# Modulation rows moved between stages, and products queued between a norm's two TensorE steps

## The chip, the core and the metric

The kernel runs on one core of a Trainium2 chip. The metric is device time of one launch in microseconds (us). A core has TensorE (PE, matrix products), VectorE (DVE), ScalarE (ACT), GpSimd (POOL) and SyncE (SP, which here only issues DMA transfers); each takes its instructions in the order in which the program has them.

## What is computed

The reference is a two-layer decoder trunk on one sequence of 1024 positions with 1024 channels, in float32. Layer 0 mixes by multi-scale pooling, layer 1 by dilated attention over one shared key/value set; after each mixer stands a gated FFN. Every sub-layer has the form

```
mod = cond @ ada_w[layer] + ada_b[layer]              # cond = silu(c)
sh1, sc1, g1, sh2, sc2, g2 = jnp.split(mod, 6, axis=-1)
h = _rmsnorm(x, norm_g) * (1 + sc) + sh
x = x + g * mixer_or_ffn(h)
```

with `_conv_ffn`: `a, v = split(h @ w_up)`, a causal 3-tap convolution on `a`, `(silu(a) * v) @ w_down`, width 2816. The key/value set has its own shift and scale from `cond @ kv_ada_w`. So there are 14 modulation rows of 1024 numbers: 0 to 5 of layer 0, 6 to 11 of layer 1, 12 and 13 of the key/value norm.

## The kernel before

Products in float32 accuracy are made of three float32r products (`whi`·`hhi`, `whi`·`hlo`, `wlo`·`hhi`); ACT rounds a weight tile to its high part, DVE subtracts for the low part (`split`, L105 to L108). Activations lie channel by position in two chunks c = 0, 1 of 512 positions.

**Stages.** Pooling layer (to 287 us); first FFN, up phase (287 to 822 us) and down phase (to 1064 us); query projection (1076 to 1310 us); value projection (1310 to 1600 us); attention with the key projection and output projection between (to 2254 us); second FFN (2267 us to the end). The first FFN and the second are the same code (`Ffn`).

**Up phase.** 22 pairs of weight tiles (`Pair`), each product done by a Strassen-like scheme in seven blocks of 12 matrix products. For the first AHEAD = 8 pairs two of the seven, which need only chunk 0 of the input, are done first (`ahead`, into a tile `ah` of the pool `t4`, stored to `ed`); `late` then makes the other operands from chunk 1 (`Norm.apply`), and `rest` does the remaining blocks for each pair in turn. `gate` (L483 on) applies convolution and gate and stores the pair's result by a GpSimd DMA (`gd<-at`, L530): one such store per pair marks the end of that pair.

**Modulation rows 5 to 13.** Each is made by `ada_dot` (L313 on): for each of 8 blocks SP loads a 512 KB tile `araw` (L321), POOL multiplies it by the conditioning row `condr` (L322), and ACT sums it in four activations with an accumulator (L325). `bg_ada` finishes the row before and starts the next. Nine rows, 72 tiles, are put into the first up phase: `bgl` is called after pair 0 and after each odd pair. `araw`, `condr` and `ah` all come from `t4`, which has 3 buffers in the FFN stages and 4 in the value projection, where the result tiles `vt` use it too.

**Norms.** `Norm.rstd` (L198 on) sums squares over channels by eight one-column TensorE products `nps` (L201), takes the root with Newton's correction on DVE (`newton`), builds four diagonals `ndg`, and spreads them over the partitions by a second TensorE product `nrs` (L208), which ACT copies to `rs`. `down_last` (L383 on) does chunk 0 of the last down products, then rstd(0) and `apply` for chunk 0, spread among the products of chunk 1, then rstd(1).

**Order.** The instructions of each engine are not run in the order of the Python code: outside the blocks under `manual_schedule` a scheduler sorts them when the program is built, with the order of the code as a preference. The order that results is fixed in the program.

## Time and profile before

| | us |
|---|---|
| median of 3 runs | 2961.41 |
| lowest, highest | 2957.07, 2967.33 |
| profiled execution | 2962.21 |
| its span, first to last instruction | 2960.4 |
| PE busy | 2757.2 (93%) |
| DVE, ACT, POOL busy | 1871.3 (63%), 1197.1 (40%), 556.5 (19%) |

The span is what the trace covers; 1.8 us of the execution lie outside it. Busy shares are averages over stages that are limited by different engines, so a stage is read by its own stretch of the trace. A PE that is busy 50 of 50 us runs one product of 512 columns each 0.227 us; PEclk is the granted TensorE clock as a share of full speed. In a row of a timeline the bracket gives the idle time before the instruction and what ended it.

### The profile page before, as it was taken

The numbers are of one execution on the slowest core, as the hardware profiler recorded it, in microseconds if no ns is written. First come the engines' busy times: TensorE is split into PE (matmuls) and PEld (weight loads), VectorE is DVE, ScalarE is ACT, GpSimd is POOL, SyncE is SP. The second block draws the span as 40 slices with busy tenths as digits, with TensorE's granted clock in tenths as the row PEclk, the third lists the DMA queues.
The fourth block names the chain that finished last, engine by engine and source line by source line (L and its number), as shares of the span: only waits on it lengthen the run. The fifth ranks groups of instructions, "written<-read, shape, count | busy, mean of one in ns | idle before, by whom it ended". The sixth has DMA issues, their size and how long they took to land.

```text
span 2960.4 us, 38089 instructions
## 1 busy us (share of the span) xinstructions
PE 2757.2 (93%) x14220; PEld 2254.0 (76%) x14220; DVE 1871.3 (63%) x3215; ACT 1197.1 (40%) x2599; POOL 556.5 (19%) x454
## 2 busy tenths in 40 slices
PE   7988978888999989989999999999988999999997
PEld 4766766666888878879999776777666888888885
DVE  6897699987665476651011565655767896666554
ACT  4634455666421143332122444544444444443112
POOL 2565154555000020000000122222142000000001
PEclk9998989999999989999999999999998999999998
DMA  7434455554342234452232233333532442225221
GB/s 298 139 131 139 160 201 180 171 171 149 131 168 100 93 122 166 167 192 100 93 99 87 74 101 110 109 103 102 159 87 100 166 139 80 84 86 206 93 71 57
DMA packets 148681, 383.76 MB, mean 130 GB/s; under 512 B 15520, under 2 KB 53392, under 8 KB 148496
## 3 DMA queue, kind: packets, MB, share of 16 engines
q1 hardware_dynamic: 109728, 292.37, 29.7%
q10 hardware_dynamic: 26496, 50.34, 4.7%
q0 software_dynamic: 12272, 38.62, 4.0%
q8 instruction: 112, 1.84, 0.2%
q14 instruction: 73, 0.60, 0.1%
HBM read 295.22 MB, written 86.05 MB: 129 GB/s over the span
## 4 chain that ended last, share of the span: by engine, by line
PE 64%; DVE 17%; DMA 9%; issue 5%; ACT 3%; POOL 2%; SPq 0%; DVEq 0%; ACTq 0%; POOLq 0%
PE dps L339 6%; PE dps L340 5%; PE dps L341 5%; PE pX L412 5%; PE pX L413 5%; PE pX L414 5%; PE vps L990 3%; PE vps L988 3%; PE vps L989 3%; DVE at L501 2%; DVE wlo L108 2%; PE pY L412 2%; PE pY L414 2%; PE pY L413 2%; PE kps L339 2%
## 5 line engine op out<-in xcount | busy, mean ns | idle before, releaser
L108 DVE TENSOR_TENSOR wlo<-wraw,whi 128x1024 fp32r<-128x1024 f32 x164 | 214.6, 1315 | 296.1 <-ACT whi L107 295.5
L339 PE MATMUL dps<-slab,whi 128*128 128x512 f32 x832 | 329.1, 397 | 9.6 <-DVE x L375 7.4
L340 PE MATMUL dps<-slab,whi 128*128 128x512 f32 x832 | 326.0, 393 | 0.0
L341 PE MATMUL dps<-slab,wlo 128*128 128x512 f32 x832 | 323.8, 393 | 0.9 <-DVE wlo L108 0.9
L375 DVE SCALAR_TENSOR_TENSOR x<-dps,mods,x 128x512 f32<-128x512 f32 x280 | 203.1, 746 | 155.7 <-PE dps L341 152.2
L107 ACT ACTIVATE whi<-wraw 128x1024 fp32r<-128x1024 f32 x164 | 169.8, 1052 | 304.2 <-PE dps L340 189.7
L1161 ACT ACTIVATE ss<-ss,ngm 128x128 f32<-128x128 f32 (+1 forms) x384 | 168.0, 439 | 191.6 <-DVE ngm L1158 178.5
L322 POOL TENSOR_TENSOR araw<-araw,condr 128x1024 f32<-128x1024 f32 x72 | 194.8, 2712 | 213.1 <-DMA araw<-in_ada_t_dram 204.8
L988 PE MATMUL vps<-whi,h 128*128 128x256 f32 x768 | 218.3, 284 | 6.1 <-ACT h L225 6.1
L990 PE MATMUL vps<-whi,h 128*128 128x256 f32 x768 | 217.7, 285 | 2.5 <-DVE h L226 2.5
L989 PE MATMUL vps<-wlo,h 128*128 128x256 f32 x768 | 217.9, 284 | 0.0
L412 PE MATMUL pX<-ht,whi 128*128 128x512 f32 x448 | 180.0, 403 | 24.7 <-ACT at L518 10.5
L339 PEld LDWEIGHTS dps<-slab,whi 128*128 128x128 f32 x832 | 158.5, 190 | 47.7 <-DVE x L375 10.3
L501 DVE SCALAR_TENSOR_TENSOR at<-at,P 128x512 f32<-128x512 f32 (+2 forms) x176 | 178.9, 1021 | 12.7 <-ACT at L498 11.4
L341 PEld LDWEIGHTS dps<-slab,wlo 128*128 128x128 f32 x832 | 158.0, 190 | 34.5 <-DVE wlo L108 1.3
L340 PEld LDWEIGHTS dps<-slab,whi 128*128 128x128 f32 x832 | 158.5, 191 | 33.6 <-issue 1.0
L414 PE MATMUL pX<-ht,wlo 128*128 128x512 f32 x448 | 178.2, 399 | 3.9 <-DVE wlo L108 3.8
L413 PE MATMUL pX<-ht,whi 128*128 128x512 f32 x448 | 178.8, 399 | 0.0
L108 DVE TENSOR_TENSOR wlo<-s,whi 128x1024 fp32r<-128x1024 f32 x112 | 150.0, 1344 | 34.6 <-ACT whi L107 34.2
L107 ACT ACTIVATE whi<-s 128x1024 fp32r<-128x1024 f32 x112 | 117.7, 1057 | 122.2 <-PE pY L413 43.5
L339 PE MATMUL kps<-h,whi 128*128 128x512 f32 x384 | 166.1, 433 | 0.0
L988 PEld LDWEIGHTS vps<-whi,h 128*128 128x128 f32 x768 | 148.4, 193 | 6.7 <-ACT h L225 6.7
(256 smaller groups left out, 6642.7 us busy)
## 6 DMA issues: line engine op xcount, KB each, us to landing
wraw<-in_wup_dram SPq DMA_DIRECT2D x104, 512.0 KB, 3.7
araw<-in_ada_t_dram SPq DMA_DIRECT2D x72, 512.0 KB, 3.9
gd<-at POOLq DMA_DIRECT2D x44, 512.0 KB, 3.5
wraw<-gd SPq DMA_DIRECT2D x44, 512.0 KB, 3.4
wraw<-in_wdn_dram SPq DMA_DIRECT2D x44, 512.0 KB, 4.1
wraw<-in_wq_dram SPq DMA_DIRECT2D x32, 512.0 KB, 4.2
xd<-x ACTq DMA_DIRECT2D x48, 256.0 KB, 2.0
ed<-ah ACTq DMA_DIRECT2D x24, 512.0 KB, 3.8
```

Source lines behind the costliest of these rows:

```text
L107: nc.scalar.activation(hi, raw, AF.Copy)
L108: nc.vector.tensor_tensor(lo, raw, hi.bitcast(F32), op=ALU.subtract)
L339: nc.tensor.matmul(ps, whi, hhi, start=first, stop=False)
L340: nc.tensor.matmul(ps, whi, hlo, start=False, stop=False)
L341: nc.tensor.matmul(ps, wlo, hhi, start=False, stop=last)
L412: nc.tensor.matmul(ps, w[0][:, k], hh, start=start and j == 0, stop=False, **kw)
L413: nc.tensor.matmul(ps, w[0][:, k], hl, start=False, stop=False, **kw)
L414: nc.tensor.matmul(ps, w[1][:, k], hh, start=False, stop=j == 3, **kw)
L501: nc.vector.scalar_tensor_tensor(t[:, lo + o:hi], a[:, lo + o - d:hi - d], pc(cw, 22 * (2 - d) + i), t[:, lo + o:hi], op0=ALU.mult, op1=AL ...
L988: nc.tensor.matmul(o, a, whi[:, k], start=kt == 0, stop=False)
L989: nc.tensor.matmul(o, a, wlo[:, k], start=False, stop=False)
L990: nc.tensor.matmul(o, b, whi[:, k], start=False, stop=kt == KT - 1)
```

## The change

Two things. First, the rows: only row 5 stays in the first up phase (after pair 12, finished after pair 17). Rows 6, 7, 12 and 13 are called after the first four sets of the down phase, rows 8 to 11 in the value projection, before every second of its first ten column groups. `condr` is loaded twice (`load_condr`), where it is first needed. Second, `rstd` becomes a generator that stops between the Newton step and the second product. In `down_last` one block of chunk 1 is called between the two for chunk 0; for chunk 1 the generator goes to the caller, which steps it after its ahead products 0 and 1.

```diff
         def rstd(self, c):
+
             ps = nbank("nps")
...
                 nc.vector.tensor_scalar(dg[:, 128 * n:128 * n + 128], ident, r[:, n:n + 1], None, op0=ALU.mult)
+            yield
             ps = nbank("nrs")
...
-            return rs
+            yield rs
...
         down(*gb, x, g, (0,), norm)
-        ap = done(0, norm.rstd(0))
+
+        def steps(c):
+            r = norm.rstd(c)
+            next(r)
+            yield
+            yield from done(c, next(r))
+
+        ap = steps(0)
         for m, _ in enumerate(down_pieces(ga[0] + gb[0], ga[1] + gb[1], x, g, (1,), norm)):
-            if m >= LEAD:
+            if m in (0, 1) or m >= LEAD:
                 next(ap)
         for _ in ap:
             pass
-
-        r = norm.rstd(1)
-
-        def late():
-            for _ in done(1, r):
-                pass
-        return late
+        return steps(1)
...
-        def up(self, late, bg=()):
-            bg = list(bg)
+        def up(self, late, bg={}):
...
                 p.ahead(ed[self.l, i])
-            late()
+                if i < 2:
+                    next(late)
+            for _ in late:
+                pass
             for i, p in enumerate(ps):
                 p.rest(self.gate(i))
-                if bg and (i == 0 or i % 2 == 1):
-                    bg.pop(0)()
-            for b in bg:
-                b()
-
-        def down(self, norm, done):
+                if i in bg:
+                    bg[i]()
+
+        def down(self, norm, done, bg=()):
...
                     down(rhs, ws, x, mod(6 * l + 5))
+                    if n < len(bg):
+                        bg[n]()
...
-    bgl = [lambda i=i: bg_ada(i) for i in (5, 6, 7, 12, 13, 8, 9, 10, 11, None)]
-    condr = tp.tile([128, 1024], F32, tag="t4", name="condr")
-    nc.sync.dma_start(condr, cvec[0, :].partition_broadcast(128))
-    nc.scalar.activation(condr, condr, AF.Silu)
+    def bg_ada_list(ids):
+        return [lambda i=i: bg_ada(i) for i in ids]
+
+    def load_condr():
+        t = tp.tile([128, 1024], F32, tag="t4", name="condr")
+        nc.sync.dma_start(t, cvec[0, :].partition_broadcast(128))
+        nc.scalar.activation(t, t, AF.Silu)
+        return t
+
     f0 = Ffn(0, tp, hs1, SL0, xd[0], gd[0])
-    f0.up(late, bgl)
-    x, late = f0.down(nrm, done1)
+
+    def first_ada():
+        nonlocal condr
+        condr = load_condr()
+        bg_ada(5)
+
+    condr = None
+    f0.up(late, {12: first_ada, 17: lambda: bg_ada(None)})
+    x, late = f0.down(nrm, done1, bg_ada_list((6, 7, 12, 13, None)))
...
+        condr = load_condr()
+        bgl = bg_ada_list((8, 9, 10, 11, None))
         for cg in range(12):
+            if cg % 2 == 0 and cg < 10:
+                bgl[cg // 2]()
             w = [wprep(wv[cg, i]) for i in range(2)]
```

The query projection and the end of the kernel step `late` in the same way as `up`. What the scheduler makes of it stands in the two programs.

POOL in the first up phase. `araw` is a modulation tile's product, a `gd` row the store that ends a pair. Before, the stretch around the stores of pairs 14, 15 and 16:

```order
L530 DMA gd_555<-at_4547 128x1024
L322 TENSOR_TENSOR araw_4540<-araw_4540,condr 128x1024
L322 TENSOR_TENSOR araw_4815<-araw_4815,condr 128x1024
L322 TENSOR_TENSOR araw_4822<-araw_4822,condr 128x1024
L322 TENSOR_TENSOR araw_4829<-araw_4829,condr 128x1024
L322 TENSOR_TENSOR araw_4836<-araw_4836,condr 128x1024
L530 DMA gd_555<-at_4679 128x1024
L322 TENSOR_TENSOR araw_4843<-araw_4843,condr 128x1024
L322 TENSOR_TENSOR araw_4850<-araw_4850,condr 128x1024
L322 TENSOR_TENSOR araw_4857<-araw_4857,condr 128x1024
L322 TENSOR_TENSOR araw_4864<-araw_4864,condr 128x1024
L530 DMA gd_555<-at_4871 128x1024
```

There the last products stand ahead of the store of pair 16 (`at_4871`). POOL now, around the stores of pairs 9, 10 and 11:

```order
L533 DMA gd_555<-at_3412 128x1024
L324 TENSOR_TENSOR araw_6238<-araw_6238,condr 128x1024
L324 TENSOR_TENSOR araw_6245<-araw_6245,condr 128x1024
L324 TENSOR_TENSOR araw_6252<-araw_6252,condr 128x1024
L324 TENSOR_TENSOR araw_6259<-araw_6259,condr 128x1024
L324 TENSOR_TENSOR araw_6266<-araw_6266,condr 128x1024
L533 DMA gd_555<-at_3544 128x1024
L533 DMA gd_555<-at_3676 128x1024
```

Products stand before the stores of pairs 0 to 16 in the program before (6, 3, 3, 3, 4, 3, 4, 2, 5, 5, 5, 5, 5, 5, 5, 5 and 4: 72) and before those of pairs 0 to 10 in the changed one (5, 3, 3, 3, 3, 3, 5, 1, 6, 3 and 5: 40). These 40 are all five rows 5, 6, 7, 12 and 13: none of them lies among the products of the down phase, though the code calls four rows from there. The other 32 lie in the value projection.

PE at the norm of chunk 1 ahead of the query projection. `dps` is the last down product, `pX` an ahead product. Before:

```order
L341 MATMUL dps_7288<-slab_6964,wlo_6972 128x512
L201 MATMUL nps_7317<-ones,sq_7157 128x1
L201 MATMUL nps_7317<-ones,sq_7174 128x1
...
L208 MATMUL nrs_7339<-ndg_7334,ones 128x512
L412 MATMUL pX_7349<-hb_7196,whi_7345 128x512
```

There nothing stands between the last `dps`, the eight `nps` and `nrs`. PE now, the same place; the twelve rows of `pX_7086<-hb_6941`, of `pX_7143<-hb_6941`, of `pX_7086<-hb_6965` and of `pX_7143<-hb_6965` are shown by one each:

```order
L343 MATMUL dps_7055<-slab_6727,wlo_6735 128x512
L417 MATMUL pX_7086<-hb_6941,wlo_7083 128x512
...
L202 MATMUL nps_7115<-ones,sq_6894 128x1
L417 MATMUL pX_7143<-hb_6941,wlo_7140 128x512
...
L417 MATMUL pX_7086<-hb_6965,wlo_7083 128x512
L202 MATMUL nps_7115<-ones,sq_6933 128x1
...
L417 MATMUL pX_7143<-hb_6965,wlo_7140 128x512
L210 MATMUL nrs_7172<-ndg_7132,ones 128x512
L415 MATMUL pX_7205<-hb_6941,whi_7201 128x512
```

Four blocks of 12 products now stand ahead of `nrs` where none stood, and 12 of them ahead of the first `nps`. The norms ahead of the two up phases have the same pattern. For chunk 0 (three of the four norms) the 12 products of one block now lie between the first `nps` and the other seven; `nrs` still follows the last `nps` at once. The last norm of chunk 1, at the end of the kernel, is as it was.

SP at the start of the value projection; `hkx` is an input of the norm's second scaling, `wraw` a weight tile, `vslab` an input of the attention. Before, the last of the `hkx` loads and what follows:

```order
L971 DMA hkx_9095<-xd_553 128x512
L971 DMA hkx_9100<-xd_553 128x512
L971 DMA hkx_9105<-xd_553 128x512
L103 DMA wraw_9974<-in_wv_dram 128x1024
L103 DMA wraw_9980<-in_wv_dram 128x1024
L1034 DMA vslab_11733<-vd 128x8x128
```

There only weight tiles follow. SP now, the same place:

```order
L991 DMA hkx_8863<-xd_553 128x512
L323 DMA araw_8898<-in_ada_t_dram 128x1024
L991 DMA hkx_8868<-xd_553 128x512
L323 DMA araw_8905<-in_ada_t_dram 128x1024
L323 DMA araw_8912<-in_ada_t_dram 128x1024
L323 DMA araw_8919<-in_ada_t_dram 128x1024
L323 DMA araw_8926<-in_ada_t_dram 128x1024
L103 DMA wraw_9915<-in_wv_dram 128x1024
L103 DMA wraw_9921<-in_wv_dram 128x1024
```

Four modulation tiles now stand ahead of the next weight tiles; the tile before `hkx_8868`, three others and the conditioning row stand among the eight `hkx` loads of chunk 1.

## Rows read from the trace of the kernel before

**Rows 1.** Stretches, both up phases: PE, PEld, DVE, ACT, POOL busy (instructions), clock, DMA

```profile
287.00:823.00 536.00, 464.68 (x1886) 368.79 (x1885) 438.94 (x458) 306.12 (x834) 207.46 (x94) 0.94 0.49 165
...
2267.00:2697.00 430.00, 428.67 (x1885) 353.62 (x1884) 319.42 (x436) 193.58 (x258) 11.64 (x22) 1.00 0.34 117
```

**Rows 2.** Timeline of TensorE, first product of each ahead phase: start, duration

```profile
286.93 1.42 PE L412 MATMUL pX<-hb,whi 128*128 128x512 f32 x1
...
2266.67 1.42 PE L412 MATMUL pX<-hb,whi 128*128 128x512 f32 x1
```

**Rows 3.** Timeline of GpSimd, first FFN: stores of pairs 7, 10, 16, 21

```profile
511.13 0.58 POOL L530 DMA_DIRECT2D gd<-at  x1 [6.18 <-DVE at L528]
...
583.75 0.59 POOL L530 DMA_DIRECT2D gd<-at  x1
...
735.45 0.59 POOL L530 DMA_DIRECT2D gd<-at  x1 [3.90 <-DVE mods L330]
...
822.29 0.53 POOL L530 DMA_DIRECT2D gd<-at  x1 [18.20 <-DVE at L529]
```

**Rows 4.** Timeline of GpSimd, second FFN: stores of pairs 7, 10, 16, 21

```profile
2432.86 0.53 POOL L530 DMA_DIRECT2D gd<-at  x1 [9.73 <-DVE at L528]
...
2487.33 0.53 POOL L530 DMA_DIRECT2D gd<-at  x1 [18.69 <-DVE at L529]
...
2600.62 0.54 POOL L530 DMA_DIRECT2D gd<-at  x1 [18.78 <-DVE at L529]
...
2696.62 0.53 POOL L530 DMA_DIRECT2D gd<-at  x1 [18.38 <-DVE at L529]
```

**Rows 5.** Busy time per engine, two stretches of the first up phase

```profile
287.00:350.00 63.00, 57.29 (x239) 45.90 (x238) 44.87 (x61) 29.87 (x43) 0.00 (x0) 0.96 0.40 135
350.00:511.00 161.00, 130.15 (x501) 101.58 (x501) 147.69 (x151) 91.38 (x280) 81.00 (x35) 0.90 0.55 185
```

**Rows 6.** VectorE groups by shape, 400 to 740 us: count, busy, mean ns

```profile
L108 DVE TENSOR_TENSOR wlo<-s,whi 128x1024 fp32r<-128x1024 f32 x30 | 50.3, 1685 | 14.8 <-ACT whi L107 14.8
...
L501 DVE SCALAR_TENSOR_TENSOR at<-at,P 128x512 f32<-128x512 f32 x30 | 45.6, 1521 | 0.6 <-ACT at L498 0.5
```

**Rows 7.** The same two groups, 2400 to 2690 us (second FFN)

```profile
L108 DVE TENSOR_TENSOR wlo<-s,whi 128x1024 fp32r<-128x1024 f32 x29 | 35.4, 1220 | 2.1 <-ACT whi L107 2.1
...
L501 DVE SCALAR_TENSOR_TENSOR at<-at,P 128x512 f32<-128x512 f32 x30 | 22.4, 748 | 1.4 <-ACT at L498 1.0
```

**Rows 8.** The page's costliest groups: the modulation products on GpSimd

```profile
L322 POOL TENSOR_TENSOR araw<-araw,condr 128x1024 f32<-128x1024 f32 x72 | 194.8, 2712 | 213.1 <-DMA araw<-in_ada_t_dram 204.8
```

**Rows 9.** ScalarE groups, 350 to 740 us: the sums of those products

```profile
L325 ACT ACTIVATE araw<-araw 128x256 f32<-128x256 f32 x288 | 116.0, 404 | 71.0 <-POOL araw L322 63.1 <-DVE mods L329 6.1 <-DVE mods L330 1.8
L325 ACT ACTIVATION_READ_ACCUMULATOR araw<-araw 128x1 f32 x288 | 53.9, 187 | 0.0
```

**Rows 10.** Timeline of TensorE, norm ahead of the query projection, chunk 1

```profile
1063.64 0.39 PE L341 MATMUL dps<-slab,wlo 128*128 128x512 f32 x1
1066.14 0.38 PE L201 MATMUL nps<-ones,sq 128*128 128x1 f32 x2 [2.11 <-POOL sq L195]
1068.97 3.15 PE L201 MATMUL nps<-ones,sq 128*128 128x1 f32 x14 [2.44 <-DVE sq L195]
1074.53 2.07 PE L208 MATMUL nrs<-ndg,ones 128*128 128x512 f32 x2 [2.41 <-DVE ndg L206]
1075.61 1.41 PE L412 MATMUL pX<-hb,whi 128*128 128x512 f32 x1
```

**Rows 11.** Timeline of TensorE, the same norm's chunk 0

```profile
1034.90 1.87 PE L201 MATMUL nps<-ones,sq 128*128 128x1 f32 x14 [1.36 <-DVE sq L195]
```

**Rows 12.** Busy time per engine, start and rest of the value projection

```profile
1310.00:1340.00 30.00, 23.15 (x164) 21.84 (x165) 21.76 (x32) 12.44 (x18) 0.00 (x0) 0.89 0.64 240
1340.00:1600.00 260.00, 260.00 (x2156) 259.47 (x2156) 29.40 (x24) 51.51 (x70) 1.83 (x5) 1.00 0.29 97
```

**Rows 13.** The page's DMA issues: size and microseconds to landing

```profile
araw<-in_ada_t_dram SPq DMA_DIRECT2D x72, 512.0 KB, 3.9
```

8 lines of the change are left out of this document (6 added, 2 removed).

## The prediction

> **What bounds the kernel now.** I read busy time by stretches first, because the kernel holds the same code twice: the first and the second FFN run the same up phase. TensorE executes 1886 and 1885 instructions in them, but the first takes 536 us and the second 430 [rows 1]. In the second, TensorE is busy 428.67 of 430 us: that phase is at its bound. In the first it is busy 464.68 of 536, so some 106 us are lost, and what stands beside it and not beside the second are the 72 modulation products: POOL is busy 207 us against 12, ACT 306 against 194, and DVE, which has no work for them to speak of, 438.94 against 319.42 [rows 1].
>
> Next, where in the phase this is lost. I count each pair's store from the first ahead product (286.93 and 2266.67 us [rows 2]) and subtract: the first FFN is behind the second by 224.2 - 166.2 = 58.0 us at pair 7, 296.8 - 220.7 = 76.2 at pair 10, 448.5 - 334.0 = 114.6 at pair 16, 535.4 - 430.0 = 105.4 at the last pair [rows 3, 4]. The loss grows as long as products are issued (43 stand before the store of pair 10, the last before that of pair 16) and then stops; 9.2 us even come back, since stores lag behind TensorE while the other engines are full.
>
> How a product costs time shows in the DVE rows. The same subtraction takes 1685 ns beside the products and 1220 without, the same convolution step 1521 against 748 [rows 6, 7]. Over the phase DVE is busy 119.5 us longer for the same work, 1.66 us for each product, which itself takes 2.71 us on POOL [rows 8]. Between 350 and 511 us DVE is busy 147.69 of 161 us [rows 5]: there it is the bound. Later ACT adds to it: a product's sums take it (116.0 + 53.9) / 72 = 2.36 us, and it stands idle for 63.1 us until POOL delivers [rows 9], with results of TensorE queued behind it.
>
> The third place is the norm. After the last down product at 1063.64 us TensorE waits 2.11 us for a sum of POOL, 2.44 for one of DVE, 2.41 for the diagonals, and begins the next product at 1075.61 [rows 10]: 11.7 us without one, counted from 1063.87, and three of the four norms of chunk 1 can be filled, as the order shows.
>
> **The change part by part.**
>
> *Products taken out of the first up phase.* By the order on POOL, 40 stay, at the same density as before and in the first half; the last stands before pair 10. The 43 up to there cost 76.2 us, so 40 cost 70.9. After them the phase should run like the second FFN's, and the 9.2 us come back as they did: 61.7 us lost in place of 105.4, a gain of 44. Lower end: nothing comes back, 34. Upper end: each product costs the phase's mean, 105.4 / 72 = 1.46 us, and 32 of them 47. I take 44, because the loss by pairs is read where these products stand.
>
> *The conditioning row.* It held one of three `t4` buffers while the ahead products ran; now it comes after them. TensorE lost at most 63 - 57.3 = 5.7 us there [rows 5]. Between 0 and 5.7 I take 3.
>
> *Norms, chunk 1.* 48 ahead products of 0.227 us now lie inside, 10.9 us. The first 12 (2.7 us) cover the wait of 2.11, the next 24 that of 2.44, the last 12 that of 2.41. The small products themselves stay: 0.4, about 1.6 at full rate and 1.1 for the spread, some 3.1 us. So 8.6 us are gained, and the first product after the wait, which took 1.41 instead of 0.39 [rows 10], gives back part of 1: 9 us. What is late next: the last `nps` comes behind 36 products (8.2 us), so the scale `rs`, and with it the operands of chunk 1, some 2 us later, which the rest of the ahead phase covers where DVE has room. For the query projection I take the 9. In the first FFN DVE is the bound right behind this place [rows 5], and moving TensorE forward does not move DVE: 3, between 0 and 9. In the second FFN DVE has 110 us of room over the phase [rows 1], less in its first pairs: 6, between 3 and 9. Together 18, between 12 and 27.
>
> *Norms, chunk 0.* The 12 products lie ahead of seven of the `nps`, not ahead of `nrs`: they cover the wait for DVE's sum, 1.36 us in the norm shown [rows 11], and leave the one for the diagonals. Three such places: 3 us, between 0 and 4.
>
> *Products added to the value projection.* From 1340 to 1600 us TensorE is busy all the time, DVE 29.4 and ACT 51.5 of 260 us, POOL not at all [rows 12]. 32 products add 87 us on POOL and 32 x 2.36 = 76 on ACT, which leaves ACT at half. The cover is TensorE's own stream with weights loaded ahead and eight result banks; without it a product would cost its 1.46 us. So the steady part costs nothing, but the start does: TensorE already waits there (23.15 of 30 us [rows 12]), ACT makes the operands, and SP now loads the conditioning row and four tiles among the eight inputs of chunk 1, while ACT's sums stand among those operands. A tile lands 3.9 us after its issue [rows 13]. I take two landings, 8 us, between 0 and 47 (32 x 1.46).
>
> What DVE shows here bears on one rule. The Trainium skill, "SBUF — State Buffer", section "Who interferes with whom", says that a VectorE instruction with two SBUF inputs and a GpSimd instruction that reads SBUF exclude one another for a whole instruction. By that rule alone the start of the value projection, where DVE scales from two SBUF inputs, would pay four whole products, 4 x 2.71 = 10.8 us in place of 8, and the sum would be 2905.
>
> *The rest.* The stores of the pairs on POOL wait behind fewer products; a second load of the conditioning row is in the 8 us. Attention, pooling layer and the end of the kernel are as they were.
>
> Sum: -44 - 3 - 18 - 3 + 8 = -60 against the profiled execution of 2962.2 us: 2902. That execution lies 0.8 us above the median of the runs, so it stands for them.
>
> **The rivals.**
>
> 1. *DVE keeps what TensorE gains.* For it: DVE full in the first pairs [rows 5]. Then nothing comes back after the products (34), the conditioning row gives 0, of the norms only the query projection's 9 arrive, and the 8 are paid: 2962 - 35 = 2927. Against: after pair 16 the time did come back. Chance 0.12.
> 2. *All of it arrives.* Upper ends throughout and a free value projection: 47 + 5.7 + 27 + 4 = 84, 2878. For it: 260 of 260 us busy there. Against: TensorE waits at that stage's start. Chance 0.12.
> 3. *The products keep their price where they go.* 47 in place of 8: 2941. Against: ACT and DVE are nearly empty there [rows 12]. Chance 0.08.
> 4. *Slower: the load queue of the value projection.* SP takes its transfers in order; a tile waits for a `t4` buffer, and the weights behind it wait too. Of four buffers the conditioning row holds one, the result tiles one or two. If one is left throughout, a product takes its landing, POOL and ACT in single file, 3.9 + 2.7 + 2.4 = 9.0 us; 32 take 287, and 24 weight tiles in the same queue some 94: 381 us for a stage of 290, which with the 68 gained elsewhere gives 2962 - 68 + 91 = 2985. It decides only if two of twelve column groups (2 x 290 / 12 = 48 us) cannot take their share, eight products, that is from 6.0 us per product on; with two buffers they take 4.5. Chance 0.02.
> 5. *The change does what its code says and not what the order shows:* four rows in the down phase, 8 products left in the up phase. 64 x 1.46 = 93 in place of 44 would give 2853. The order is what runs; chance 0.01.
>
> **How the numbers follow.** The forecast has the other 0.65; its own range is 2888 to 2918. The range of 2876 to 2930 takes in rivals 1 and 2 and leaves out 3 to 5, 0.11, and the tails. A measurement of this kernel tells about 0.3%, 9 us, from no change: only rival 4 is slower by that (0.02); of rival 3 a part, 0.01, might come near no change; faster 0.97.
>
> **What would show it right or wrong.** In the profile of the changed kernel the stores of pairs 11 to 21 should be 19 us apart, and the up phase some 490 to 505 us long counted from the first ahead product, which now starts inside the norm; DVE's convolution step should be back at 750 ns behind pair 11. At the norm of chunk 1 the wait of TensorE for the diagonals should be gone, and ahead products should stand where it was. In the value projection TensorE should be busy without a break once it has started. Wrong would be: stores after pair 11 still 25 us apart; waits for weights inside the value projection; a first up phase no shorter than 515 us.

## The result: 2892.85 us, 2.4% less

| | before | change |
|---|---|---|
| median of the runs compared, us | 2963.6 (4 runs) | 2892.85 (2884.02 to 2893.51, 4 runs) |
| ratio, 95% interval | | 0.9757 [0.973, 0.9783] |
| profiled execution, its span | 2962.21, 2960.4 | 2893.38, 2891.6 |

The forecast was 2902 (2876 to 2930), 60 us less than the profiled execution of before; 69 to 71 us came. The profile of the changed kernel, view by view as it was read before:

Busy time by stretches, the first and the second FFN's up phase (PE, PEld, DVE, ACT, POOL busy with instructions, PEclk, DMA share, GB/s):

```profile
282.00:768.00 486.00, 448.21 (x1906) 364.00 (x1907) 392.00 (x465) 259.50 (x584) 121.54 (x63) 0.97 0.45 154
2194.00:2629.00 435.00, 431.47 (x1901) 356.19 (x1900) 330.68 (x457) 199.36 (x267) 13.53 (x24) 1.00 0.35 122
```

The first up phase is shorter by 50 us than in [rows 1]: PE is busy 448 of 486 us, and DVE 392 in place of 438.94 for the same code. POOL has lost 86 us of work there. The second is as full as before.

First ahead product of both FFNs on TensorE's timeline, then GpSimd's stores of pairs 7, 10, 11, 16 and 21 of the first FFN and 21 of the second:

```profile
282.35 0.47 PE L415 MATMUL pX<-hb,whi 128*128 128x512 f32 x1 [0.94 <-DVE x L377]
...
2194.16 0.39 PE L415 MATMUL pX<-hb,whi 128*128 128x512 f32 x1
...
487.22 0.59 POOL L533 DMA_DIRECT2D gd<-at  x1 [2.13 <-DVE at L531]
...
563.22 0.59 POOL L533 DMA_DIRECT2D gd<-at  x1 [5.17 <-DVE mods L332]
...
579.43 0.53 POOL L533 DMA_DIRECT2D gd<-at  x1 [15.61 <-DVE at L532]
...
670.49 0.53 POOL L533 DMA_DIRECT2D gd<-at  x1 [18.50 <-DVE at L532]
...
766.95 0.53 POOL L533 DMA_DIRECT2D gd<-at  x1 [18.57 <-DVE at L532]
...
2628.67 0.53 POOL L533 DMA_DIRECT2D gd<-at  x1 [17.77 <-DVE at L532]
```

Counted from the first ahead product, as with [rows 2 to 4], pair 7 is 204.9 - 171.7 = 33.2 us behind the second FFN (store of its pair 7 at 2365.82; 58.0 before), pair 10 is 55.1 behind (its pair 10 at 2419.98; 76.2 before), and the last pair 484.6 - 434.5 = 50.1 (105.4 before). From pair 11 on the stores are (766.95 - 579.43) / 10 = 18.8 us apart.

VectorE's groups by shape in the same kernel, 400 to 563 us (products run) and 580 to 765 us (none left):

```profile
L108 DVE TENSOR_TENSOR wlo<-s,whi 128x1024 fp32r<-128x1024 f32 x16 | 25.4, 1585 | 5.9 <-ACT whi L107 5.9
...
L504 DVE SCALAR_TENSOR_TENSOR at<-at,P 128x512 f32<-128x512 f32 x16 | 20.4, 1272 | 0.3 <-ACT at L501 0.2
...
L108 DVE TENSOR_TENSOR wlo<-s,whi 128x1024 fp32r<-128x1024 f32 x16 | 19.5, 1221 | 1.4 <-ACT whi L107 1.4
...
L504 DVE SCALAR_TENSOR_TENSOR at<-at,P 128x512 f32<-128x512 f32 x20 | 15.0, 748 | 0.3
```

Beside products the subtraction takes 1585 ns and the convolution step 1272; behind the last one both are where [rows 7] had them, 1221 and 748.

The norm of chunk 1 ahead of the query projection, TensorE's timeline (start, duration, bracket: wait and what ended it):

```profile
1006.01 0.39 PE L343 MATMUL dps<-slab,wlo 128*128 128x512 f32 x1
...
1006.24 0.39 PE L415 MATMUL pX<-hb,whi 128*128 128x512 f32 x1
...
1011.44 0.59 PE L202 MATMUL nps<-ones,sq 128*128 128x1 f32 x2 [2.31 <-POOL sq L195]
...
1018.81 1.62 PE L202 MATMUL nps<-ones,sq 128*128 128x1 f32 x14
...
1023.45 1.13 PE L210 MATMUL nrs<-ndg,ones 128*128 128x512 f32 x2 [0.17 <-DVE ndg L207]
```

The first ahead product follows the last down product at once. The wait for GpSimd's sum is 2.31 us, no shorter than the 2.11 of [rows 10], although 12 products now stand before it; the one of 2.44 is gone and the one of 2.41 is 0.17.

Busy time by stretches, start and rest of the value projection:

```profile
1243.00:1275.00 32.00, 21.71 (x148) 20.25 (x149) 24.29 (x26) 16.03 (x38) 10.82 (x4) 0.89 0.85 316
1275.00:1305.00 30.00, 26.67 (x220) 26.27 (x220) 11.72 (x12) 16.78 (x55) 10.51 (x4) 1.00 0.59 190
1305.00:1538.00 233.00, 233.00 (x1942) 232.96 (x1942) 27.61 (x29) 83.49 (x254) 60.55 (x30) 1.00 0.43 146
```

Between 1275 and 1305 us TensorE still loses 3.3 us, where [rows 12] had none; from 1305 on it is busy without a break, with 24 of the 32 products beside it (the other 6 of GpSimd's 30 instructions are short ones of 0.3 to 0.4 us).

### The profile page after: what moved, and what is told of

Same layout as the page of the kernel before. It is cut to its first block, busy times and chain, and to the rows that moved or that the text cites. A ratio compares the mean times of both kernels' runs of the same rounds, so it can differ in the third digit from the quotient of the medians.

```text
span 2891.6 us, 38074 instructions
## 1 busy us (share of the span) xinstructions
PE 2732.7 (95%) x14220; PEld 2243.5 (78%) x14220; DVE 1832.1 (63%) x3215; ACT 1195.5 (41%) x2599; POOL 548.2 (19%) x454
## 4 chain that ended last, share of the span: by engine, by line
PE 68%; DVE 14%; DMA 8%; issue 6%; ACT 3%; POOL 2%; SPq 0%; ACTq 0%; DVEq 0%; POOLq 0%
PE pX L415 7%; PE pX L416 6%; PE pX L417 6%; PE dps L341 6%; PE dps L342 6%; PE dps L343 6%; PE vps L1014 3%; PE vps L1013 3%; PE vps L1012 3%; PE pY L415 3%; PE pY L417 3%; PE pY L416 3%; DVE at L504 2%; PE kps L341 2%; PE kps L343 1%
## 5 line engine op out<-in xcount | busy, mean ns | idle before, releaser
L324 POOL TENSOR_TENSOR araw<-araw,condr 128x1024 f32<-128x1024 f32 x72 | 187.7, 2616 | 479.1 <-DVE hkx L992 249.6
L504 DVE SCALAR_TENSOR_TENSOR at<-at,P 128x512 f32<-128x512 f32 (+2 forms) x176 | 156.2, 894 | 8.2 <-ACT at L501 6.7
L1012 PEld LDWEIGHTS vps<-whi,h 128*128 128x128 f32 x768 | 148.4, 193 | 10.0 <-ACT h L227 10.0
L1014 PEld LDWEIGHTS vps<-whi,h 128*128 128x128 f32 x768 | 147.5, 193 | 6.3 <-DVE h L228 6.2
```

Source lines behind the costliest of these rows:

```text
L504: nc.vector.scalar_tensor_tensor(t[:, lo + o:hi], a[:, lo + o - d:hi - d], pc(cw, 22 * (2 - d) + i), t[:, lo + o:hi], op0=ALU.mult, op1=AL ...
L1012: nc.tensor.matmul(o, a, whi[:, k], start=kt == 0, stop=False)
L1014: nc.tensor.matmul(o, b, whi[:, k], start=False, stop=kt == KT - 1)
```

## The experiments

To compare kernels I cut each profile at the same instructions: the first down product of the pooling layer (0), the store of the first FFN's pair 0 and of its pair 21, the last down product of the first FFN, the first and the last product of the value projection. All lengths in us; the starts and ends are those of the timelines. "First up phase" here and in what follows is counted from 0, so it includes the pooling layer's down products and the norm.

| kernel | 0 to pair 0 | 0 to pair 21: **first up phase** | to last down product | norm of chunk 1 and query | value projection |
|---|---|---|---|---|---|
| before | 229.6 | 674.7 | 241.4 | 249.3 | 283.9 |
| change | 213.2 | 615.1 | 239.1 | 242.1 | 289.4 |
| 1 rows only | 224.0 | 627.6 | 242.1 | 248.7 | 291.1 |
| 2 norms only | 214.8 | 655.6 | 239.4 | 245.3 | 282.5 |
| 3 no value rows | 211.6 | 615.6 | 240.4 | 239.3 | 282.6 |
| 4 no up rows | 203.0 | 558.8 | 239.9 | 240.8 | 290.8 |
| 5 first norm kept | 224.5 | 628.1 | 239.6 | 244.5 | 289.8 |
| 6 no multiply | 207.8 | 569.1 | 239.9 | 239.8 | 282.3 |
| 7 rows held back | 212.6 | 570.5 | 248.5 | 242.2 | 288.4 |
| 8 rows on VectorE | 211.6 | 584.1 | 239.4 | 244.2 | 281.5 |
| 9 multiply last | 209.5 | 612.0 | 238.9 | 243.6 | 294.5 |
| 10 VectorE, held back | 212.2 | 570.8 | 245.2 | 244.4 | 282.3 |
| 11 kept, 3 weight buffers | 223.7 | 579.2 | 240.0 | 254.0 | 291.2 |
| 12 kept, 4 weight buffers | 229.0 | 580.7 | 238.0 | 254.3 | 291.8 |

A stretch that no edit touches, from the store of pair 0 to that of pair 21 in the second FFN, lies between 354.0 and 357.6 us in all fourteen, so a difference under 4 us between two kernels says little here. Runs 1 to 4, 5 to 8 and 9 to 12 shared a chip each with runs of before, which took 2969.8, 2963.88 and 2963.96 us there; ratios are against those.

### 1. The rows alone

The code of the change with the old norms: `rstd` without the first `yield`, `late` after all ahead products.

```diff
-            yield
             ps = nbank("nrs")
...
-        ap = steps(0)
+        ap = done(0, norm.rstd(0))
...
-        return steps(1)
+        return done(1, norm.rstd(1))
...
                 p.ahead(ed[self.l, i])
-                if i < 2:
-                    next(late)
```

> The rows are moved as in the change; the norms stay as they were (both TensorE steps back to back). Theory 1, the terms of the prediction as they stand: 44 + 3 out of the first up phase, 8 back in the value projection, 39 us less than before: about 2924. Theory 2, read from the trace of the change, where the first up phase came out shorter than forecast by some 8 us: the rows alone carry that too, some 50 us out of the first up phase and 5.5 back in the value projection: about 2917, and the store of pair 0 then comes 8 us or more earlier, counted from the first ahead product. Theory 3: the extra 8 us come from the norm, whose ahead products let the weights of the first pairs be loaded sooner; then this kernel gains 39 or less, 2924 to 2930, and the store of pair 0 is as late as before (90 us behind the first ahead product).

2921.32 us, ratio to before 0.9839 [0.982, 0.9857]. The first up phase is 674.7 - 627.6 = 47.1 us shorter, which is the 44 + 3 of the prediction, and 5.6 of them have come by the store of pair 0. The length lies at theory 1 and only 3 us from theory 2, which this doesn't exclude, nor do the times: 48.5 us less by the medians on this chip, 34.6 by the spans of the profiled executions. The store of pair 0 comes earlier than theory 3 has it and later than theory 2 has it. The value projection pays 7.2.

### 2. The norms alone

All rows where they were, the norms as in the change.

```diff
-    condr = None
-    f0.up(late, {12: first_ada, 17: lambda: bg_ada(None)})
-    x, late = f0.down(nrm, done1, bg_ada_list((6, 7, 12, 13, None)))
+    condr = load_condr()
+    f0.up(late, dict(zip((0, 1, 3, 5, 7, 9, 11, 13, 15, 17), bg_ada_list((5, 6, 7, 12, 13, 8, 9, 10, 11, None)))))
+    x, late = f0.down(nrm, done1)
...
-        condr = load_condr()
-        bgl = bg_ada_list((8, 9, 10, 11, None))
...
-            if cg % 2 == 0 and cg < 10:
-                bgl[cg // 2]()
```

> The norms are changed as in the change; all 72 products stay in the first up phase. Theory 1, the terms of the prediction: 18 + 3 us less than before, about 2941, of it some 3 in the first up phase, 10 before the query projection, 7 before the second FFN. Theory 2: the same. Theory 3 (the norm also brings the first pairs forward): 12 us more, about 2929, nearly all of it in the first up phase. Rival 1 of the prediction (VectorE keeps what TensorE gains): the first up phase ends no earlier and only the query projection and the second FFN gain, about 2946.

2927.07 us, ratio 0.9866 [0.9847, 0.9884]: 42.7 us less by the medians on this chip, twice the forecast of theory 1 (21), and 36.1 less by the spans. The first up phase gains 674.7 - 655.6 = 19.1 us where the prediction had 3 and 1, and 14.8 of them are there at the store of pair 0. So theory 3 holds in the main: the norm brings the first pairs forward by more than the rows do.

Do the two parts add? In the first up phase they overlap, 47.1 + 19.1 = 66.2 alone against 59.6 together. By spans of the profiled executions they add, 34.6 + 36.1 = 70.7 us against 68.8 (2960.4 less 2925.8, 2924.3 and 2891.6); by medians against the runs of before on their chip the two give 48.5 + 42.7 = 91 against 71. Before took 6 us more on that chip than on the two others, and the spans set executions on that chip against one of before that was not taken with them, so neither settles it to better than some 10 us.

### 3. and 4. Products left out

Run 3 leaves out rows 8 to 11 and with them the second load of the conditioning row, run 4 the other five rows; the edit of run 3:

```diff
-        condr = load_condr()
-        bgl = bg_ada_list((8, 9, 10, 11, None))
+        for i in (8, 9, 10, 11):
+            nc.vector.tensor_copy(mod(i), ada_bias(i))
...
-            if cg % 2 == 0 and cg < 10:
-                bgl[cg // 2]()
```

> The changed kernel without rows 8 to 11: their 32 products are left out of the value projection, and the bias stands for these rows. Theory: the products cost only the start of that stage, 5 to 8 us, since TensorE is busy without a break behind it: about 2886. Rival a: they cost their price of the up phase, 47 us: about 2846. Rival b: the start waits for its own inputs anyway and the products cost nothing: 2893.

2891.19 us, ratio 0.9735 [0.9721, 0.975], against 0.9757 [0.973, 0.9783] of the change. The two intervals overlap, so the times rule out rival a (2846) and not rival b (2893). The stage itself tells them apart: the value projection takes 282.6 us, 6.8 less, and in the six kernels without GpSimd's multiplications there it takes 281.5 to 283.9, in the others 288.4 to 294.5. The theory holds: the products cost the start of that stage, and nothing from 1305 us on, where the change has TensorE busy 233 of 233 us.

> The changed kernel without rows 5, 6, 7, 12 and 13: the 40 products that stay in the first up phase are left out, and the bias stands for these rows. Theory: the products are all that sets the first up phase apart from the second (50 us at the last store in the changed kernel): about 2843, stores 19 us apart from the first pair on. Rival: part of the difference is something else at the start of the first FFN (its first weights, its norm), so that 15 to 20 us stay: about 2860.

2837.7 us, ratio 0.9553 [0.9537, 0.9569]. The up phase without products, busy time by stretch:

```profile
279.00:711.00 432.00, 431.92 (x1911) 357.09 (x1910) 326.23 (x452) 195.12 (x262) 12.42 (x23) 1.00 0.37 123
```

TensorE is busy all the time; from pair 0 to pair 21 this first FFN takes 558.8 - 203.0 = 355.8 us, its second 357.6. So the products are the whole difference between the two FFNs, and 40 of them cost 615.1 - 558.8 = 56.3 us, 1.41 each (the prediction had 61.7 for them).

### 5. The old norm in the first FFN alone

```diff
+            if self.l == 0:
+                next(late)
+                next(late)
             for i, p in enumerate(ps[:AHEAD]):
                 p.ahead(ed[self.l, i])
-                if i < 2:
+                if self.l == 1 and i < 2:
                     next(late)
```

(with a stop of the generator more, so that `nrs` runs and `apply` doesn't).

> The changed kernel, but in the first FFN alone the norm of chunk 1 runs to its end before the first ahead product, as before the change. Theory, from the two runs of one part each: in this place the norm is worth 12 us beside 40 products, because the ahead products empty the split weight tiles sooner and the loads behind them restart sooner: 12 us slower than the change, about 2905, and the store of pair 0 some 10 us later, counted from the start of the pooling layer's down products. The term as the prediction had it (VectorE is full behind this place and keeps the gain): 3 us slower, about 2896, with the store of pair 0 within 3 us.

2902.21 us, ratio 0.9795 [0.9781, 0.9808], 9 us more than the change by the medians and 11 by the ratios, whose intervals just overlap. The up phase is 628.1 - 615.1 = 13.0 us longer, the store of pair 0 comes 11.3 us later. The theory's size holds and the prediction's 3 us fall; the reason that the theory gives, weight loads that restart sooner, this run doesn't show.

Busy time in the first 63 us from the first ahead product, of this run and then of the change (whose second line is the rest of the first eight pairs):

```profile
289.00:352.00 63.00, 63.00 (x269) 51.41 (x268) 46.11 (x62) 32.33 (x45) 0.00 (x0) 0.97 0.46 156
```

```profile
282.00:345.00 63.00, 62.57 (x281) 51.47 (x282) 54.86 (x81) 37.67 (x52) 2.27 (x2) 1.00 0.58 201
345.00:487.00 142.00, 117.84 (x469) 92.85 (x468) 133.62 (x144) 82.47 (x260) 72.20 (x33) 0.93 0.56 194
```

TensorE has no gap to speak of in this stretch in either, at a granted clock of 0.97 here and 1.00 in the change. VectorE has 46.11 of 63 us here and 54.86 in the change. [rows 5] had 44.87 for the kernel before. So VectorE was not full behind the norm: it had some 17 us to spare, and in the change the norm's own steps go into that time beside the ahead products, which here stand behind them. What that brings shows at TensorE's first long wait for VectorE behind the ahead products, here and in the change:

```profile
359.97 0.79 PE L418 MATMUL pY<-hb,whi 128*128 128x512 f32 x1 [5.64 <-DVE v L522]
```

```profile
350.77 0.50 PE L415 MATMUL pY<-hb,whi 128*128 128x512 f32 x1 [2.52 <-DVE v L519]
```

Counted from 0 of the table, the first ahead product comes 139.0 - 130.5 = 8.5 us sooner in the change, the product before this wait 203.6 - 196.0 = 7.6, and the one behind it 209.6 - 198.9 = 10.7: VectorE is further on as well, and TensorE waits 3.1 us less for it. That is 10.7 of the 11.3 us at the store of pair 0. VectorE is nearly full only from some 60 us on (133.62 of 142 us). In the kernel before TensorE lost time on top of that, 57.29 of 63 us busy at a granted clock of 0.96.

### 6. The multiplication left out

```diff
-            nc.gpsimd.tensor_tensor(raw, raw, condr, op=ALU.mult)
```

> The changed kernel with the multiplication on GpSimd left out of every modulation product; loads, sums and order stay. Theory: of the 56 us that 40 products cost the first up phase (measured by leaving them out), most are VectorE's, slowed by GpSimd beside it; without it VectorE's subtraction takes 1220 ns and its convolution step 750 ns throughout, and 15 us or less of the 56 stay (the sums on ScalarE): 2850 to 2860. Rival: ScalarE's sums, with results of TensorE queued behind them, are the price; then no more than 10 us are gained, 2883 or more, though VectorE's steps are short.

2836.66 us, ratio 0.9573 [0.956, 0.9586]. Loads and sums alone cost the first up phase 569.1 - 558.8 = 10.3 of 56.3 us; the multiplication is 46.0. In the value projection it is all of it: 282.3 us with tiles, conditioning row and sums in their places, 282.6 without any. VectorE at the start of that stage, scaling `hkx` and making low parts: first the change, 1245 to 1280 us, then this run, 1196 to 1231 us (count, busy, mean ns):

```profile
L992 DVE SCALAR_TENSOR_TENSOR hkx<-hkx,mods,rs 128x512 f32<-128x512 f32 x16 | 18.0, 1147 | 6.8 <-DMA hkx<-xd 6.8
L228 DVE SCALAR_TENSOR_TENSOR h<-hkx,mods,h 128x512 fp32r<-128x512 f32 x14 | 15.1, 1090 | 1.8 <-ACT h L227 1.6
```

```profile
L991 DVE SCALAR_TENSOR_TENSOR hkx<-hkx,mods,rs 128x512 f32<-128x512 f32 x16 | 11.6, 748 | 7.1 <-DMA hkx<-xd 7.1
L228 DVE SCALAR_TENSOR_TENSOR h<-hkx,mods,h 128x512 fp32r<-128x512 f32 x16 | 11.6, 749 | 6.2 <-ACT h L227 6.0
```

The same instructions take 1147 and 1090 ns beside GpSimd's products, 748 and 749 without.

### 9. The multiplication kept, behind the sums

This run was to tell apart the two ways in which GpSimd's work could reach TensorE: by slowing VectorE, or by making ScalarE wait.

```diff
-            nc.gpsimd.tensor_tensor(raw, raw, condr, op=ALU.mult)
             w = D // KQ
             for k in range(KQ):
                 nc.scalar.activation(raw[:, w * k:w * k + w], raw[:, w * k:w * k + w], AF.Copy,
                                      accum_out=q[:, m, k:k + 1])
+            nc.gpsimd.tensor_tensor(raw, raw, condr, op=ALU.mult)
```

> The changed kernel with the order inside a modulation product turned round: ScalarE sums the tile as it landed, and GpSimd multiplies it afterwards, for nothing (the rows come out without the conditioning factor). GpSimd's work stays, and ScalarE no longer waits for it. Leaving the multiplication out altogether gave back 46 of 56 us of the first up phase and all of the 7 in the value projection. Theory (GpSimd's reading slows VectorE's two-input instructions): nearly the whole price stays, first up phase 605 to 615 us from the start of the pooling layer's down products, value projection 287 to 290, time 2880 to 2893. Rival (ScalarE stands still until GpSimd delivers, and TensorE's results behind its sums wait too): the price goes as if the multiplication were left out, first up phase 570 to 580, time 2837 to 2850.

2890.62 us, ratio 0.9751 [0.9737, 0.9765]: as slow as the change. The up phase takes 612.0 us, the value projection 294.5, longer than the change's 289.4 and than the 290 that I had set as its end. Busy time of the up phase here and in run 6, then VectorE's two groups here (400 to 563 us) and in run 6 (400 to 510 us):

```profile
279.00:764.00 485.00, 448.53 (x1914) 364.10 (x1915) 392.96 (x467) 258.58 (x584) 124.70 (x63) 0.97 0.46 155
```

```profile
279.00:721.00 442.00, 435.93 (x1910) 358.69 (x1911) 328.87 (x465) 258.89 (x584) 13.12 (x23) 0.99 0.49 169
```

```profile
L108 DVE TENSOR_TENSOR wlo<-s,whi 128x1024 fp32r<-128x1024 f32 x16 | 28.4, 1773 | 1.2 <-ACT whi L107 1.2
...
L504 DVE SCALAR_TENSOR_TENSOR at<-at,P 128x512 f32<-128x512 f32 x14 | 18.7, 1337 | 0.0
```

```profile
L108 DVE TENSOR_TENSOR wlo<-s,whi 128x1024 fp32r<-128x1024 f32 x15 | 18.3, 1222 | 2.1 <-ACT whi L107 2.1
...
L503 DVE SCALAR_TENSOR_TENSOR at<-at,P 128x512 f32<-128x512 f32 x14 | 10.5, 748 | 1.1 <-ACT at L500 1.0
```

With the multiplication VectorE is busy 393 us, without it 329, for the same work; ScalarE has the same 259 in both. The multiplication costs 612.0 - 569.1 = 42.9 us for 40 products, although no sum takes its result.

That doesn't yet rule out the rival, since ScalarE still waits for GpSimd in this run, by a longer way. A tile's buffer is free for the next load only when GpSimd is done with it. ScalarE's waits before the sums in the up phase, in the change, in this run and in run 6, and the wait of the loads in this run:

```profile
ACT araw L327 <- POOL araw L324: 23.9, 15, 3.3
```

```profile
ACT araw L326 <- DMA araw<-in_ada_t_dram: 27.6, 13, 4.3
```

```profile
ACT araw L326 <- DMA araw<-in_ada_t_dram: 10.9, 11, 1.9
```

```profile
SPq L323 <- POOL araw L328: 101.5, 29, 7.2
```

What speaks against the rival is VectorE's own time. All its waits for ScalarE add up to 29.1 us here and 27.7 in run 6, those for landed weights to 19.2 and 26.2: it is longer at work, by 64 us, and doesn't wait longer. TensorE's waits that end with ScalarE do grow, from 4.3 to 19.6 us, and ScalarE in turn waits for VectorE. So the longer VectorE steps carry most of the price, and up to 15 of the 42.9 us may pass through ScalarE; no run separates that part.

### 7. The rows held back until the down phase

The order has all of rows 6, 7, 12 and 13 in the up phase, although the code calls them in the down phase. Here a 1 worked out from the first set's result is multiplied into their conditioning row, so that they can't come sooner.

```diff
...
+                condr = load_condr()
+                one = cp.tile([128, 1], F32, tag="one1", name="one1")
+                nc.vector.tensor_scalar(one, xs(x, 7, 1)[:, 0:1], 0.0, 1.0, op0=ALU.mult, op1=ALU.add)
+                nc.vector.tensor_scalar(condr, condr, one, None, op0=ALU.mult)
```

> The changed kernel with rows 6, 7, 12 and 13 held back until the first set of down products is done: their conditioning row is multiplied by a 1 that is worked out from that set's result, so the order can't bring them forward. 8 products stay in the first up phase, 32 go to the down phase. Theory: the price depends on the room beside the products; the down phase has it (VectorE 147 of 255 us, ScalarE 58 of 255), so the up phase gains 45 of 56 us and the down phase loses 0 to 8: 2848 to 2858. Rival: a product costs its 1.4 us wherever VectorE works beside GpSimd, and nothing is gained: about 2893. Rival 2: the rows come too late for the norm that needs them, and the products of the query projection wait: the down phase or the norm grows by 10 us or more, 2860 to 2880.

2857.63 us, ratio 0.9645 [0.9628, 0.9662]. The up phase gains 44.6 us, the down phase loses 9.4, a little more than I had set. The down phase:

```profile
719.00:966.00 247.00, 235.81 (x1031) 193.66 (x1030) 144.19 (x180) 102.55 (x313) 102.42 (x45) 0.99 0.49 166
```

The 9.4 us are 0.3 for each of the 32 products, where in the up phase a product costs 1.41. VectorE is busy 144 of 247 us here. The forecast holds, but room is not the whole reason for the low price. VectorE's three largest groups in the down phase, with the products (this run) and without (run 4, 710 to 949 us):

```profile
L377 DVE SCALAR_TENSOR_TENSOR x<-dps,mods,x 128x512 f32<-128x512 f32 x109 | 76.8, 744 | 41.2 <-PE dps L343 39.9 <-DMA x<-xd 1.3
L108 DVE TENSOR_TENSOR wlo<-wraw,whi 128x1024 fp32r<-128x1024 f32 x18 | 25.6, 1457 | 27.0 <-ACT whi L107 27.0
L108 DVE TENSOR_TENSOR slab<-wraw,slab 128x1024 fp32r<-128x1024 f32 x16 | 21.1, 1317 | 27.3 <-ACT slab L107 27.3
```

```profile
L377 DVE SCALAR_TENSOR_TENSOR x<-dps,mods,x 128x512 f32<-128x512 f32 x110 | 79.7, 747 | 67.1 <-PE dps L343 65.2 <-DMA x<-xd 1.7
L108 DVE TENSOR_TENSOR wlo<-wraw,whi 128x1024 fp32r<-128x1024 f32 x18 | 21.5, 1220 | 5.1 <-ACT whi L107 5.1
L108 DVE TENSOR_TENSOR slab<-wraw,slab 128x1024 fp32r<-128x1024 f32 x16 | 19.6, 1225 | 23.6 <-ACT slab L107 23.4
```

The subtractions, which read both inputs from SBUF, are stretched (1220 to 1457 ns, 1225 to 1317). The largest group isn't: it reads one input from PSUM, where TensorE's results lie, and takes 744 ns beside the products and 747 without. So 32 products lengthen these three groups by some 5 us here, 0.2 each, against 1.6 each in the up phase, where VectorE's largest groups, subtraction and convolution step, read SBUF alone: the price hangs on which VectorE instructions run beside the product as well as on VectorE's room, and this run can't part the two.

### 8. and 10. VectorE makes the products

One instruction multiplies and sums a tile; GpSimd and ScalarE have nothing to do.

```diff
-        q = cp.tile([128, 8, KQ], F32, tag="q", bufs=1, name=nm("q"))
+        q = cp.tile([128, 8, 1], F32, tag="q", bufs=1, name=nm("q"))
...
-            nc.gpsimd.tensor_tensor(raw, raw, condr, op=ALU.mult)
-            w = D // KQ
-            for k in range(KQ):
-                nc.scalar.activation(raw[:, w * k:w * k + w], raw[:, w * k:w * k + w], AF.Copy,
-                                     accum_out=q[:, m, k:k + 1])
+            nc.vector.scalar_tensor_tensor(raw, raw, 1.0, condr, op0=ALU.mult, op1=ALU.mult,
+                                           accum_out=q[:, m, 0:1])
```

> The changed kernel with each modulation product made by one VectorE instruction (multiply and accumulate) in place of GpSimd's multiplication and ScalarE's four sums. Theory: VectorE is what a product costs; in place of some 1.7 us of slowing it now pays one instruction of some 1.2 us, and ScalarE is free: a product's 1.4 us become about 1.0, 16 of 56 us gained: about 2877. Rival a: ScalarE's sums were the larger part; then 40 us or more are gained: 2853 or less. Rival b: VectorE takes its instructions in order and now waits for tiles that have not landed: no gain or slower, 2893 to 2920.

2854.6 us, ratio 0.9631 [0.9617, 0.9644]: 31.0 us off the up phase and 7.9 off the value projection. The new instruction in this run, 400 to 530 us, with what it reads out behind it, and the subtraction beside it:

```profile
L324 DVE SCALAR_TENSOR_TENSOR araw<-araw,condr 128x1024 f32<-128x1024 f32 x24 | 29.2, 1229 | 0.3 <-DMA araw<-in_ada_t_dram 0.3
...
L324 DVE DVE_READ_ACCUMULATOR araw<-araw,condr 128x1 f32 x24 | 2.2, 93 | 0.0
...
L108 DVE TENSOR_TENSOR wlo<-s,whi 128x1024 fp32r<-128x1024 f32 x16 | 19.5, 1226 | 0.0
```

A product takes VectorE 1.32 us and costs TensorE (584.1 - 558.8) / 40 = 0.63. My estimate of 1.0, which scaled the price by VectorE's time (1.2 against 1.7 us), was too high. The time comes near that of rival a (2853 or less), but run 6, where the sums stay and cost at most 10.3 us with the loads, speaks against ScalarE's sums as the larger part. Rival b, that VectorE waits for tiles, isn't seen: the idle time before the 24 instructions is 0.3 us.

Both together, run 8 with the rows held back as in run 7:

> Two runs put together: each product is one VectorE instruction, and rows 6, 7, 12 and 13 are held back until the first set of down products is done. Theory: the up phase gains as much as with the rows held back or a little more (45 to 50 us), the down phase, which lost 9 us with GpSimd's products, loses 0 to 4, and the value projection pays nothing (8 us less): 2837 to 2845. Rival: VectorE, which takes its instructions in order, waits for tiles in the down phase and the norm comes late: 9 us or more lost there, about 2850.

2843.89 us, ratio 0.9592 [0.9578, 0.9607], the shortest of the kernels with nothing left out, 120.1 us less than before, where the change is 70.8 less. The up phase is as long as in run 7, the value projection pays nothing, the down phase 6.1 us, between the theory and its rival. Its busy times:

```profile
720.00:966.00 246.00, 239.00 (x1043) 196.49 (x1042) 173.28 (x246) 48.89 (x56) 18.95 (x13) 0.98 0.50 170
```

VectorE is busy 173 of 246 us with the 32 products, and 135 of 239 in the down phase of the change. The same instruction that cost TensorE 0.63 us in the up phase costs 6.1 / 32 = 0.19 here, where VectorE has room.

### 11. and 12. A fourth buffer for weights

A try at the cause of run 5's 13 us. Rows, norm and `t4` are as the first expectation says; then `wraw` gets four buffers in place of three.

```diff
-        for tag, bufs in (("t4", 3), ("t2", 5), ("s", 2), ("h5", 1), ("l5", 1)):
+        for tag, bufs in (("t4", 2), ("t2", 5), ("s", 2), ("h5", 1), ("l5", 1)):
...
-        raw = wp.tile([128, 1024], F32, tag="wraw", bufs=3, name=nm("wraw"))
+        raw = wp.tile([128, 1024], F32, tag="wraw", bufs=4, name=nm("wraw"))
```

> Reference for the next: the changed kernel without the 40 products of the first up phase, with the first FFN's norm as before the change, and with two buffers in place of three in the pool t4 of the FFN stages (room for a fourth weight buffer). Theory: the norm term shows without products too: the store of pair 0 comes 8 to 13 us later than in the kernel without those products and with the new norm (203 us from the start of the pooling layer's down products): 211 to 216. If the first pairs are VectorE's without products too, it comes within 3 us of 203.

> As the run before, with four buffers for landed weight tiles in place of three. Theory: behind the norm the first pairs wait for weights, whose loads stand still while TensorE does (a buffer comes free when the tile's low part is made, and that needs room that TensorE frees); with one more tile landed ahead the store of pair 0 comes 4 to 8 us earlier than with three buffers. Rival: the wait is VectorE's work on the operands of chunk 1, not the loads: within 1.5 us of the run with three.

One execution each, 2875.69 and 2869.62 us. Pair 0 is stored at 223.7 us, later than expected, and with the fourth buffer at 229.0, later still: the theory that loads alone hold up the first pairs finds no support. VectorE's waits in the first 63 us from the first ahead product (waited for: us in total, times, longest), three buffers, then four:

```profile
DVE wlo L108 <- ACT whi L107: 7.8, 3, 6.7
DVE s L458 <- DMA wraw<-in_wup_dram: 6.0, 3, 2.5
```

```profile
DVE wlo L108 <- ACT whi L107: 15.5, 5, 7.1
...
DVE s L458 <- DMA wraw<-in_wup_dram: 1.0, 1, 1.0
```

The wait for landed weights falls from 6.0 to 1.0 us, and the one for ScalarE's high parts grows from 7.8 to 15.5. Something behind the loads is late too. The order that the scheduler makes differs between the two kernels, and the two buffers of `t4` may add to it, so more than this can't be read from them. What the transfers show in either case (run 5, then the change; each number the GB/s of a fortieth of the 63 us from the first ahead product):

```profile
GB/s 0 0 0 0 0 0 0 0 0 36 317 289 354 153 182 140 265 304 304 395 271 0 0 166 166 138 354 174 0 134 33 104 369 192 23 257 349 273 224 276
```

```profile
GB/s 117 299 185 398 271 245 0 333 294 99 317 289 0 0 0 0 39 281 390 304 257 94 257 57 0 166 330 336 99 263 304 0 83 250 62 259 339 312 346 364
```

With the old norm nothing is moved for the first 14 us; with the new one transfers run at once and pause later. How 8.5 us at the first ahead product become 11.3 at the store of pair 0 is read from TensorE's wait under run 5. Which of the norm's steps, operands or weights VectorE was late with there, and whether the 13.0 at pair 21 is more than the 11.3, stays open.

## Why the prediction was right, and where it wasn't

| term of the sum | forecast | measured |
|---|---|---|
| products out of the first up phase, conditioning row | -44 - 3 | -47.1 alone (run 1); -40.5 where the norms come first (run 2 to change) |
| norm of chunk 1, first FFN | -3 (0 to 9) | **-13.0** (run 5 to change); -19.1 with all rows there (run 2) |
| norm of chunk 1, query projection | -9 | -7.2 |
| norm of chunk 1 and of chunk 0, second FFN | -6 - 1 | -8.1 (last product of the value projection to the store of pair 0, 743.35 to 735.27) |
| other norms of chunk 0 | -2 | -2.3 ahead of the query projection, -1.1 at the end |
| products into the value projection | +8 (0 to 47) | +5.5; +6.8 by run 3 |

With 4.3 us that this execution was late before the pooling layer's down products (151.87 against 147.59 us, code that the change doesn't touch; the runs lie between 147.2 and 151.9), the lengths from profile to profile give 4.3 - 59.6 - 2.3 - 7.2 + 5.5 - 8.1 - 1.1 = -68.5 us; the span fell by 68.8. The total lies inside the range, but the norms of chunk 1 together gained some 27 to 28 us, the very upper end of the 12 to 27 that the prediction gave them.

**The step that failed** is "In the first FFN DVE is the bound right behind this place [rows 5], and moving TensorE forward does not move DVE: 3, between 0 and 9". [rows 5] has two lines. The second, 350 to 511 us, has VectorE at 147.69 of 161; the place in question lies in the first, where it is at 44.87 of 63. I carried the reading of one stretch over into its neighbour. Run 5 measured 13.0 us, above the upper end, and run 2 19.1 with all products still there; moving TensorE forward by 8.5 us did move VectorE, which had 54.86 us of work behind it in the first 63 us in place of 46.11, and for which TensorE then waited 2.52 us in place of 5.64. That is most of the 9 to 11 us by which the gain was larger than forecast. Rival 1, which rests on the same reading, falls with it.

**The products' price** was right as a mechanism and in size. VectorE's steps with both inputs in SBUF are stretched beside GpSimd's products, and the multiplication costs 43 to 46 of 56.3 us (run 9 and the change against run 6). The prediction put part of the price on ScalarE's sums and its waits for GpSimd; loads and sums cost 10.3 us (run 6), and of the waits run 9 shows only that they carry some 15 us at most. That after the last product the phase runs like the second FFN's, and a little comes back, holds: 5.0 us (55.1 to 50.1) in place of 9.2. In the length of the phase, 490 to 505 us expected, the 485 reached show the norm again. At the query projection 7.2 us came in place of 9: the 12 products ahead of the first `nps` were to cover the wait for GpSimd's sum, and 2.31 us of it are still there.

**The value projection** had about the right size for a wrong reason, which is luck. The 8 us stood for two landings in SP's queue. Run 6 has all the tiles in that queue and pays nothing; the price is the multiplication beside VectorE's scaling, 1147 against 748 ns. The start paid 6.8 us by run 3 and 294.5 - 282.6 = 11.9 in run 9. The rule that the prediction set against it, the Trainium skill, "SBUF — State Buffer", section "Who interferes with whom", that a VectorE instruction with two SBUF inputs and a GpSimd instruction that reads SBUF exclude one another, was the better reason, and the estimate of four whole products that goes with it, 10.8 us, lies between the two. Runs 6 and 9 agree with it in kind, and so does run 7: the VectorE instruction with one input in PSUM takes 744 ns beside the products, 747 without. Rival 3 (the full price in the new place) and rival 4 (the queue) fall with run 3: behind the start 24 products cost nothing. Rival 2 (all of it arrives) falls here and at the query projection. The sign that TensorE would be busy without a break once that stage has started was met only from 1305 us on; it still lost 3.3 us in the 30 us before.

**Rival 5** asked what the code would do if the order let it. The order decided, as forecast; run 7 shows that the code's own places would have been worth 35 us more by the medians against before (106 against 71).

## What to carry to other kernels

Work handed to GpSimd isn't free because GpSimd is idle: in a stretch where VectorE is nearly full and mostly reads both inputs from SBUF each such product cost 1.4 us of TensorE's time; in one where VectorE had 40% to spare and took one input mostly from PSUM it cost 0.3. As one VectorE instruction it cost 0.6 in the first stretch and 0.2 in the second. Where a scheduler sorts the instructions, moving a call in the code doesn't move the work; look at the order, and where a place matters make it a dependency. When a term rests on an engine being full, read it from the very stretch in which the moved work lies. And an experiment that takes one wait away may move it elsewhere: look at the waits of its trace before calling a rival dead.

## What was not expected of the hardware

A multiplication on GpSimd whose result no other instruction takes lengthened the phase by 1.07 us for each (42.9 / 40), though GpSimd was busy only a quarter of it. Beside GpSimd's multiplications VectorE's instructions with two inputs in SBUF grew longer, and the scaling that takes one input from PSUM stayed as it was (744 ns in run 7, 747 in run 4). And VectorE's multiply with an accumulator over 1024 elements takes 1229 ns and 93 to read out, no longer than a plain subtraction of that shape (1226), and leaves its neighbours their time; it fills VectorE nearly as much as GpSimd's product stretches it (1.32 us, against 1.66 by the prediction's rows), and yet costs TensorE only about half: 0.63 us with its load, against 1.07 to 1.15 for GpSimd's multiplication alone and 1.41 with loads and sums. ScalarE's waits, which one VectorE instruction does away with, may be part of the difference; that wasn't settled.
